# A hybrid diffusion layer on one core: the convolution's tiles are issued beside the last two RWKV pairs, and the order of issue is worked out with other durations

## The chip, the cores and the metric

One core of a Trainium2 chip runs the whole program. The metric is the device time of one execution, in microseconds (us); the time before is 1356.08 us, the median of three runs (1353.59 to 1361.63). The rows below come from one further execution that was profiled.

## What is computed

One layer of a hybrid backbone for 128 context and 512 latent tokens (T = 640 columns here, width D = 1024, all in float32). The reference, cut to what matters:

```python
xn = RMSNorm(x)*(1+sc1)+sh1
rkv, glu_in, gate_r, gate_c = split(xn @ w_in)
y_r = rwkv_branch(xn, rkv)      # two scans (forward, backward) per head, 8 heads of 64
y_c = conv_branch(glu_in)       # a * sigmoid(gt) -> depthwise conv of width 31 -> LayerNorm -> silu -> @ w_out_conv
x  += g1 * ((sigmoid(gate_r)*y_r + sigmoid(gate_c)*y_c) @ w_o)
x  += g2 * (relu(xn2 @ mlp_w1)**2 @ mlp_w2)
return RMSNorm(x)
```

## The kernel before

Activations lie with channels on the 128 partitions and tokens along the free axis. A dense product is done in split precision: a 128x512 piece of weights is split into a high part (ScalarE, `wh`) and a low part (VectorE, `wl`), and each of its four 128x128 blocks gives three matmuls of 320 columns (xh with wh, xl with wh, xh with wl). These are the rows `ps_mm<-xh_t,wh_t` and their like; one dense job is 48 of them, in two halves of the tokens.

The middle of the program is one loop over *lanes* (L1350 to L1364 in before), generators that record instructions for TensorE, VectorE and ScalarE in an order fixed by a small estimate: `now` is TensorE's time, `free` the other engines', `cost_v`, `cost_a` and `cost_g` the estimated durations, `mm` advances `now` by each matmul. A lane whose time has come is resumed, the more urgent first (table `URGENT`). Where none is ready, one matmul of the dense stream (`fill`) is recorded. `hungry` lets the dense stream go first where the estimate sees TensorE's clock about to fall. SyncE's DMA queue is not ordered by this loop. On the chip each engine works through its own list in order and waits where an operand is not there.

The lanes: `lora2_all`, `ada_all` (late modulation columns), and for each of four head pairs p `prep` (operands of the scan), `solve` (`gram` and `inverse`, long on VectorE), `builder` (five groups of scan matrices: a first block of matmuls that ends in bank `ps_t`, then one on `ps_a`, then one on `ps_a` and `ps_b`), `scan` (`chain`: ten steps in bank `ps_ad`, then `post`, the normalisation of the pair's output, whose result goes to DRAM as `out{p}`). `out_branch` reads the four `out{p}` back, splits them, and makes the side "r". `conv_all` is the convolution's lane: it waits until the gated inputs of the convolution are in DRAM, then `conv_tile` works on five tiles of 128 tokens: four transposes, for each 64-token row a matmul into frequencies (`cf_w`, 512 columns) and two VectorE products, an inverse transform (`cf_w`, 64 output rows), mean and variance, transposes back, tanh and scaling. Every one of these matmul groups writes the single bank `ps_t`, as do parts of the build, of the inverse and of `post`. The tiles' result makes the side "c".

The dense stream takes jobs in the order of `todo`: input projections, gates 8 to 15, two jobs of side "c", gates 0 to 7, then the four jobs of side "r" among the other two of "c". A job of a side that is not ready is passed over. After the loop come `w_o`, the MLP and the last norm, which the change leaves as they are.

In before, `conv_all` waits until pair 3 is inverted (`while 3 not in inverted`), and takes its tiles' space from the inverse (tags `prod`, `Nb`, `Gf`, `Gt`, `E`).

Of the kernel before, what the change touches and what calls it, by code (L numbers as in the profile page):

```python
# [17 lines left out]
P = 128  # L18
D = 1024
KD = D // P  # L20
T = 640
# [37 lines left out]
RAWS, SPLITS, SWITCH, EXTRA = ["ZB", "L"], ["N1"], 1, 0  # L59
# [11 lines left out]
TICK, ENTRY, QUOTA, CREDIT, DEBT = 3.413, 3060, 1.55, 200, 6000  # L71
# [7 lines left out]
def hybrid_step(ctx: ExitStack, tc: tile.TileContext, I, O):  # L79
# [115 lines left out]
    def mm(out, lhsT, rhs, start=True, stop=True, **kw):  # L195
        PE.matmul(out=out, lhsT=lhsT, rhs=rhs, start=start, stop=stop, **kw)  # L196
        cyc = math.prod(rhs.shape[1:]) * (1 if rhs.dtype == F32R else 2 if "is_transpose" in kw else 4)
        m = math.prod(lhsT.shape[1:])
        overlap = 128 // m if m < 128 else 128 // rhs.shape[0]
        cols = cyc * rhs.shape[0] / 128 * (1 if rhs.dtype == F32R else 0.5)  # L200
        gated["cols"] += cols
        gated["burst"] -= cols
        gated["credit"] = min(gated["credit"] + cols, CREDIT)
        kind = (m, rhs.shape[0], rhs.dtype)
        if kind != gated["kind"]:
            advance(now[0] + SWITCH * gated["drain"] / (2400 if gated["warm"] else 1200))
        gated.update(kind=kind, drain=0 if rhs.dtype == F32R else max(cyc, 256) - max(cyc / overlap, 64))
        advance(now[0] + (max(cyc / overlap, 64) + EXTRA) / (2400 if gated["warm"] else 1200))
        ready[out.name] = ("P", now[0] + SEM / 2)
        last[0] = now[0]  # L210
# [779 lines left out]
    def solve(p):  # L990
# [4 lines left out]
        inverted.add(p)  # L995

# [92 lines left out]
    def conv_all():  # L1089
# [6 lines left out]
        while 3 not in inverted:  # L1096
            yield 0.5
        ew = wt([P, 2 * P + W], "prod")[0:32]
        DMA.dma_start(out=ew[:, 0:2 * P], in_=I["ce"])
        DMA.dma_start(out=ew[:, 2 * P:], in_=I["cwb"])  # L1100
        yield 3.0
        for j in range(2):
            ps = bank("t")
            mm(ps, ew[:, P * j:P * j + P], ew[:, 2 * P:])
# [5 lines left out]
        us, tok = wt([P, 2, 4, P], "prod"), wt([P, 2, W], "Nb")  # L1110
        prods = [wt([P, 2, W], tag) for tag in ("Gf", "Gt")]

        def load(i):
            if i < 5:
                for j in range(4):
                    DMA.dma_start(out=us[:, i % 2, j], in_=dram(f"glu{j}")[:, P * i:P * i + P])

        load(0)
        yield 2.5
# [3 lines left out]
        places.extend(("Gf", "Gt"))  # L1123
        sides["c"] = Side(un, 8, merge_c, ("kS", "kS"))
        yield 2.5
        ready_sides.add("c")

    def conv_tile(i, u, tok, prods, un):

        ut, yn = tok[:, 0], tok[:, 1]  # L1130
        ps = bank("t")
        for j in range(4):
            mm(ps[:, P * j:P * j + P], u[:, j], ident)
        A.activation(ut, ps, AF.Copy)
        yield
        for r in range(2):
# [3 lines left out]
            V.scalar_tensor_tensor(out=prods[r][:, 0], in0=ps, scalar=cf[:, P + 384:P + 385], in1=cg[:, 0], op0=ALU.add, op1=ALU.mult)  # L1140
            V.tensor_tensor(out=prods[r][:, 1], in0=ps, in1=cg[:, 1], op=ALU.mult)
            yield
        ps = bank("t")
        for j in range(2):
            for r in range(2):
                o = P + 192 * j + 64
                if i < 4:
                    mm(ps[64 * r:64 * r + 64], cf[:, o:o + 64], prods[r][:, j], j == 0, j == 1)
                else:
                    mm(ps, cf[:, o - 64 * r:o - 64 * r + P], prods[r][:, j], (j, r) == (0, 0), (j, r) == (1, 1))  # L1150
        y = wt([P, W], "E")
        A.activation(y, ps, AF.Copy)
        yield
# [5 lines left out]
        V.tensor_scalar(out=yn, in0=y, scalar1=mv[:, 0:1], scalar2=r1, op0=ALU.subtract, op1=ALU.mult)  # L1159
        yield  # L1160
        ps = bank("t")
        for j in range(4):
            mm(ps[:, P * j:P * j + P], yn[:, P * j:P * j + P], ident)
        z, th = wt([P, 4, P], "E"), ut.rearrange("p (j t) -> p j t", j=4)
# [5 lines left out]
        V.scalar_tensor_tensor(out=z, in0=th, scalar=1.0, in1=z, op0=ALU.add, op1=ALU.mult)  # L1170
        yield
        h, l = (un[:, j, :, P * i:P * i + P] for j in range(2))
        A.activation(h, z, AF.Copy)
        yield
        V.tensor_tensor(out=l, in0=z, in1=h.bitcast(F32), op=ALU.subtract)
        yield
# [76 lines left out]
    def ada_all():  # L1253
        e = wt([P, 4, P], "ade")
        for c in range(16, 48):
            yield from ada_late(c, e)

# [383 lines left out]
```

## Time and profile before

| what | us |
|---|---|
| median of the runs | 1356.08 |
| the profiled execution | 1359.46 |
| its span, first to last instruction | 1357.4 |
| from 150 us to the last step of the last pair's chain | 521.4 |
| from there to the first product of a side | 93.3 |
| side products, to the first `w_o` matmul in another bank | 56.4 |
| `w_o`, MLP, last norm | 536.3 |

The stretches are cut at 150.0, 671.4, 764.7 and 821.1 us. In a row of the timeline stand start, duration, engine, source line, operation, output and inputs, and in brackets the idle time of the engine before it and what ended it. PEclk is TensorE's granted clock as a share of 2.4 GHz: 0.50 is the lower level, 1.2 GHz.

### The profile page before, as it was taken

Reading aid. Unit: us, or ns where it says so; the run is one execution under the profiler, and the core shown is the slowest. Engines: PE = TensorE matmul, PEld = TensorE weight load, DVE = VectorE, ACT = ScalarE, POOL = GpSimd, SP = SyncE. Lnnn points to the kernel's source line nnn. Section 1 sums busy time; section 2 is a strip of 40 time slices with the busy share of each in tenths; the row PEclk is TensorE's granted clock in tenths of the full one; section 3 lists DMA queues with packets and bytes.
Section 4 is the critical chain, followed back from the end, with each engine's and each line's share of the span. In section 5 each row is a group of like instructions: output and inputs, shape, how many; then the busy total and the mean of one; then the engine's idle time right before and its main releaser. Section 6 shows DMA issues by size and latency. Waiting matters only on the chain.

```text
span 1357.4 us, 29973 instructions
## 1 busy us (share of the span) xinstructions
PE 1228.3 (90%) x12790; PEld 1098.3 (81%) x12790; DVE 662.8 (49%) x1354; ACT 491.2 (36%) x1093; POOL 29.2 (2%) x30
## 2 busy tenths in 40 slices
PE   8999889989889998998755599999999999999996
PEld 5767787768778876886532589999999999999996
DVE  5426655656556454633432366574443443344344
ACT  4555244325433543343311323344431341242130
POOL 0000000010000000000000000000000000000000
PEclk9999889998989998998955699989999999999998
DMA  9475422324213212430100385212222222222222
GB/s 373 152 227 174 132 77 97 125 93 136 82 54 106 65 49 71 130 101 27 48 27 0 103 253 199 94 37 66 78 78 78 72 76 71 78 78 78 72 76 78
DMA packets 77780, 136.20 MB, mean 100 GB/s; under 512 B 10768, under 2 KB 27824, under 8 KB 77648
## 3 DMA queue, kind: packets, MB, share of 16 engines
q1 hardware_dynamic: 77648, 134.30, 30.1%
q8 instruction: 100, 1.64, 0.5%
q14 instruction: 32, 0.26, 0.1%
HBM read 113.03 MB, written 21.23 MB: 99 GB/s over the span
## 4 chain that ended last, share of the span: by engine, by line
PE 82%; DVE 6%; DMA 4%; ACT 4%; issue 4%; SPq 0%; POOL 0%; POOLq 0%; DVEq 0%; ACTq 0%
PE ps_mm L196 42%; PE ps_b L196 21%; PE ps_t L196 11%; PE ps_a L196 5%; PE ps_ad L196 3%; DMA adar_s<-in_adaw 2%; ACT S_w L108 1%; DVE Gt_w L108 1%; ACT Nb_w L108 1%; DMA z<-tmp 1%; DVE E_w L108 1%; DVE prod_w L108 1%; ACT tmp L108 1%; DVE Y_w L108 0%; DVE wl_t L108 0%
## 5 line engine op out<-in xcount | busy, mean ns | idle before, releaser
L196 PE MATMUL ps_mm<-xh_t,wh_t 128*128 128x320 f32 x680 | 226.5, 333 | 1.1 <-ACT tmp L108 1.0
L196 PE MATMUL ps_mm<-xh_t,wl_t 128*128 128x320 f32 x680 | 223.3, 328 | 1.2 <-DVE wl_t L108 1.2
L196 PE MATMUL ps_mm<-xl_t,wh_t 128*128 128x320 f32 x680 | 222.6, 327 | 0.0
L108 DVE TENSOR_TENSOR wl_t<-wr_t,wh_t 128x512 fp32r<-128x512 f32 x152 | 104.4, 687 | 108.9 <-ACT wh_t L108 108.8
L108 ACT ACTIVATE wh_t<-wr_t 128x512 fp32r<-128x512 f32 x152 | 95.5, 629 | 149.6 <-PE ps_b L196 106.6
L196 PEld LDWEIGHTS ps_mm<-xh_t,wh_t 128*128 128x128 f32 x680 | 133.5, 196 | 17.7 <-issue 12.0
L196 PEld LDWEIGHTS ps_mm<-xh_t,wl_t 128*128 128x128 f32 x680 | 133.7, 197 | 12.3 <-issue 8.1
L196 PEld LDWEIGHTS ps_mm<-xl_t,wh_t 128*128 128x128 f32 x680 | 134.0, 197 | 10.0 <-issue 7.8
L196 PE MATMUL ps_mm<-ARGH_t,wh_t 128*128 128x320 f32 x284 | 78.3, 321 | 11.7 <-ACT wh_t L108 11.0
L108 ACT ACTIVATE tmp<-ps_mm 128x320 f32<-128x320 f32 x80 | 34.9, 436 | 110.1 <-PE ps_mm L196 95.6
L196 PE MATMUL ps_mm<-ARGH_t,wl_t 128*128 128x320 f32 x212 | 67.6, 319 | 0.0
L196 PEld LDWEIGHTS ps_mm<-ARGH_t,wh_t 128*128 128x128 f32 x284 | 53.2, 199 | 12.5 <-ACT wh_t L108 11.3
L108 ACT ACTIVATE mwh<-wr_t 128x512 fp32r<-128x512 f32 x49 | 31.1, 635 | 74.0 <-PE ps_b L196 70.2
L108 DVE TENSOR_TENSOR tmp<-tmp 128x320 f32<-128x320 f32 x64 | 31.3, 489 | 43.2 <-ACT tmp L108 43.1
L108 DVE TENSOR_TENSOR mwl<-wr_t,mwh 128x512 fp32r<-128x512 f32 x49 | 33.9, 691 | 37.9 <-ACT mwh L108 37.8
L108 DVE SCALAR_TENSOR_TENSOR ARGH_t<-ps_mm,mod_t,ARGH_t 128x320 f32<-128x320 f32 (+2 forms) x45 | 22.6, 512 | 59.5 <-PE ps_mm L196 59.5
L196 PE MATMUL ps_mm<-xl,wh_t 128*128 128x320 f32 x140 | 44.1, 315 | 0.0
L196 PE MATMUL ps_b<-xl,wh_t 128*128 128x320 f32 x140 | 43.2, 309 | 0.0
L196 PE MATMUL ps_b<-ARGH_t,wl_t 128*128 128x320 f32 x140 | 43.0, 307 | 0.0
L196 PE MATMUL ps_b<-ARGH_t,wh_t 128*128 128x320 f32 x140 | 43.0, 307 | 0.0
L196 PEld LDWEIGHTS ps_mm<-ARGH_t,wl_t 128*128 128x128 f32 x212 | 41.7, 196 | 0.4 <-DVE wl_t L108 0.4
L196 PE MATMUL ps_ad<-M_w,S_w 128*64 128x64 f32 x320 | 19.1, 244 | 24.5 <-ACT S_w L108 23.0
(375 smaller groups left out, 3011.6 us busy)
## 6 DMA issues: line engine op xcount, KB each, us to landing
wr_t<-in_w SPq DMA_DIRECT2D x224, 256.0 KB, 2.6
adl_w<-in_adal SPq DMA_DIRECT2D x64, 256.0 KB, 3.3
adar_s<-in_adaw SPq DMA_DIRECT2D x16, 512.0 KB, 8.4
ARGH_t<-in_x SPq DMA_DIRECT2D x8, 640.0 KB, 6.2
z<-tmp SPq DMA_DIRECT2D x32, 160.0 KB, 2.9
gate<-tmp SPq DMA_DIRECT2D x32, 160.0 KB, 1.8
tA_t<-z SPq DMA_DIRECT2D x8, 320.0 KB, 3.2
ath_t<-z SPq DMA_DIRECT2D x8, 320.0 KB, 4.4
```

Of the source, the lines that this page charges most:

```text
L108: return f(*args, **kw)
L196: PE.matmul(out=out, lhsT=lhsT, rhs=rhs, start=start, stop=stop, **kw)
```

## The change

The convolution's tiles start earlier, as soon as pair 2 is prepared, pair 3's r and k are projected and the late modulation is done (`modulated`). Their space now comes from buffers that are free then (`kS`, `rS`, `adl`, `ade`). Each 64-token row of a tile has its own inverse transform right after its products, so that the two halves of the output, which stood next to one another in TensorE's order, now stand apart. A tile's result goes to DRAM (`conv{j}`); a new lane `conv_branch` reads it back once pair 2 is built, splits it and makes side "c". The bank stays `ps_t`. In the estimate, the costs of VectorE and ScalarE, of a fp32r matmul (`EXTRA`, 31 cycles more) and of going between fp32 and fp32r (`ENTER`, `LEAVE`) are changed, the time from a matmul to its reader is doubled (`SEM` for `SEM / 2`), and `QUOTA` goes from 1.55 to 1.25.

```diff
-TICK, ENTRY, QUOTA, CREDIT, DEBT = 3.413, 3060, 1.55, 200, 6000
+TICK, ENTRY, QUOTA, CREDIT, DEBT = 3.413, 3060, 1.25, 200, 6000
...
+EXTRA, ENTER, LEAVE = 31, 250, 220
...
     def cost_v(name, n, src, kw):
-        return 0.07 + 0.06 * aps_(kw, "scalar", "scalar1") + n / 960
+        return 0.155 + n / (480 if name == "tensor_tensor_scan" else 550 if name == "transpose" else 960)
...
-        return (0.08 if src[0].space == PSUM else 0.16) + 0.093 * aps_(kw, "scale", "bias") + n / 1400
+        return (0.16 if src[0].space == PSUM else 0.19) + 0.093 * aps_(kw, "scale", "bias") + n / 1180
...
-            advance(now[0] + SWITCH * gated["drain"] / (2400 if gated["warm"] else 1200))
+            enters = (rhs.dtype == F32R) - (gated["kind"] is not None and gated["kind"][2] == F32R)
+            advance(now[0] + (gated["drain"] + (0, ENTER, LEAVE)[enters]) / (2400 if gated["warm"] else 1200))
...
-        while 3 not in inverted:
+        while 2 not in prepared or (0, 3) not in rk or (1, 3) not in rk or not modulated:
             yield 0.5
...
-        while 2 not in built or 3 not in operated:
-            yield 0.3
-        un = st([P, 2, 4, T], "ARGH", 2, F32R)
+        pr = [wt([P, W], "adl", 2) for _ in range(2)]
         for i in range(5):
-            load(i + 1)
-            yield from conv_tile(i, us[:, i % 2], tok, prods, un)
+            for j in range(4):
+                DMA.dma_start(out=u[:, P * j:P * j + P], in_=dram(f"glu{j}")[:, P * i:P * i + P])
+            yield 2.5
+            yield from conv_tile(i, u, ut, pr)
+        spawn(conv_branch(), URGENT["branch"])
...
         for r in range(2):
...
             yield
+            ps = bank("t")
+            at, n = (lo, 64) if i < 4 else (slice(0, P), P)
+            for j in range(2):
+                o = P + 192 * j + 64 - (0 if i < 4 else 64 * r)
+                mm(ps[at], cf[:, o:o + n], pr[j], j == 0, j == 1)
...
+        for j in range(4):
+            DMA.dma_start(out=dram(f"conv{j}")[:, P * i:P * i + P], in_=z[:, j])
...
+    def conv_branch():
+
+        while 2 not in built or 3 not in operated:
+            yield 0.3
+        un = st([P, 2, 4, T], "ARGH", 2, F32R)
+        for j in range(4):
+            t = st([P, T], f"ath{j % 2}")
+            DMA.dma_start(out=t, in_=dram(f"conv{j}"))
+            yield 2.5 if j == 0 else 0.5
+            split(un[:, 0, j, :], un[:, 1, j, :], t)
+            yield "V"
+        sides["c"] = Side(un, 8, merge_c, ("kS", "kS"))
```

TensorE's list at the end of the last pair. Before, from the last two chain steps (`ps_ad`) on: `Y_w`, `pa_t` and `rh_t` belong to `post` of pair 3, `prod_w`, `Nb_w` and `cf_w` to the convolution, `ARGH_t` with `wh_t` to side "c".

```order
L196 MATMUL ps_ad<-S_w,M_w 64x64 x4
L196 MATMUL ps_ad<-M_w,S_w 64x64 x4
L196 MATMUL ps_t<-cst_t,Nb_w 128x128 x4
L196 MATMUL ps_t<-Y_w,cst_t 64x320 x4
L196 MATMUL ps_t<-cst_t,pa_t 128x2 x5
L196 MATMUL ps_t<-cst_t,prod_w 128x128 x4
L196 MATMUL ps_t<-cst_t,rh_t 64x128 x10
L196 MATMUL ps_t<-Nb_w,cf_w 128x512 x2
L196 MATMUL ps_t<-Gf_w,cf_w 64x512
L196 MATMUL ps_t<-Gt_w,cf_w 64x512
```

Two further tiles of the same kind follow before the first product of side "c". The same place now (`Gt_w` holds weights of side "c" here; the last row is the first product of side "r"):

```order
L197 MATMUL ps_mm<-ARGH_t,Gt_w 128x320 x5
L197 MATMUL ps_ad<-S_w,M_w 64x64 x4
L197 MATMUL ps_ad<-M_w,S_w 64x64 x4
L197 MATMUL ps_mm<-ARGH_t,Gt_w 128x320 x8
L197 MATMUL ps_t<-Y_w,cst_t 64x320 x2
L197 MATMUL ps_mm<-ARGH_t,Gt_w 128x320 x4
L197 MATMUL ps_t<-Y_w,cst_t 64x320 x2
L197 MATMUL ps_t<-cst_t,pa_t 128x2 x5
L197 MATMUL ps_t<-cst_t,rh_t 64x128 x10
L197 MATMUL ps_mm<-ARGH_t,wh_t 128x320 x2
```

No matmul of the convolution is left behind the chain; 84 of the 96 matmuls of the first two "c" jobs stand ahead of its last step, 12 among `post`.

TensorE's list at the inverse transform of a tile. Before, beside pair 3, with the two halves of the tile next to one another (`Gf_w`, `Gt_w` are their products) among gates:

```order
L196 MATMUL ps_mm<-xl_t,wh_t 128x320
L196 MATMUL ps_mm<-xh_t,wl_t 128x320
L196 MATMUL ps_t<-Gf_w,cf_w 64x512
L196 MATMUL ps_t<-Gt_w,cf_w 64x512
L196 MATMUL ps_t<-Gf_w,cf_w 64x512
L196 MATMUL ps_t<-Gt_w,cf_w 64x512
L196 MATMUL ps_mm<-xh_t,wh_t 128x320
```

Now, beside the build of pair 2 (rows `ps_t<-ARGH_t` are the end of the build's first block, `ps_a` its second block):

```order
L197 MATMUL ps_t<-cst_t,ARGH_t 64x64
L197 MATMUL ps_t<-ARGH_t 64x64
L197 MATMUL ps_t<-adl_w,cf_w 64x512 x2
L197 MATMUL ps_mm<-xl_t,wh_t 128x320
```

One half of the tile stands alone, and here, as at three more places, a step of the convolution stands directly behind the build's first block, where five or six dense matmuls stood in before.

## Rows read from the trace of the kernel before

**Rows 1.** The page: busy time, share of the span and instructions of each engine.

```profile
PE 1228.3 (90%) x12790; PEld 1098.3 (81%) x12790; DVE 662.8 (49%) x1354; ACT 491.2 (36%) x1093; POOL 29.2 (2%) x30
```

**Rows 2.** Windows: length, busy of PE, PEld, DVE, ACT, POOL, PEclk, DMA share, GB/s.

```profile
150.00:671.40 521.40, 470.52 (x7614) 401.49 (x7612) 282.77 (x593) 214.90 (x533) 18.49 (x16) 0.95 0.27 88
671.40:764.70 93.30, 46.67 (x133) 23.17 (x131) 30.97 (x59) 16.92 (x33) 3.97 (x4) 0.56 0.06 18
764.70:821.10 56.40, 53.74 (x337) 52.00 (x338) 33.59 (x66) 14.25 (x27) 0.00 (x0) 0.94 0.77 239
821.10:1357.40 536.30, 523.08 (x3553) 521.70 (x3552) 249.33 (x505) 170.39 (x333) 3.41 (x4) 0.98 0.24 79
```

**Rows 3.** Timeline of TensorE behind the chain's last step, 668 to 714 us.

```profile
670.97 0.45 PE L196 MATMUL ps_ad<-M_w,S_w 128*64 128x64 f32 x8 [0.38 <-ACT ade_t L108]
...
676.37 1.34 PE L196 MATMUL ps_t<-Y_w,cst_t 128*64 128x320 f32 x4 [3.87 <-DVE E_w L108]
...
686.47 1.98 PE L196 MATMUL ps_t<-cst_t,rh_t 128*64 128x128 f32 x16 [0.84 <-ACT Nb_w L108]
...
693.94 2.07 PE L196 MATMUL ps_t<-Nb_w,cf_w 64*128 64x512 f32 x2 [1.44 <-DVE Gf_w L108]
```

**Rows 4.** Timeline of VectorE in the same stretch: the steps of `post`.

```profile
671.77 0.29 DVE L108 TENSOR_TENSOR Y_w<-ps_ad,Y_w 128x128 f32<-128x128 f32 x1 [0.73 <-ACT Y_w L108]
...
690.02 0.35 DVE L108 SCALAR_TENSOR_TENSOR Y_w<-Y_w,par_t,ps_t 128x128 f32<-128x128 f32 x1 [0.79 <-PE ps_t L196]
...
693.80 0.88 DVE L108 SCALAR_TENSOR_TENSOR Y_w<-Y_w,par_t,pg_t 128x640 f32<-128x640 f32 x1
...
697.62 0.83 DVE L108 TENSOR_TENSOR Y_w<-Y_w,pg_t 128x640 f32<-128x640 f32 x1 [0.22 <-DMA pg_t<-g]
```

**Rows 5.** Timeline of SyncE's queue: the pair's output is stored; its landing.

```profile
698.47 0.32 SPq L1073 DMA_DIRECT2D out<-Y_w  x1
...
DMA to landing us min/median/max: 2.1/2.1/2.1
```

**Rows 6.** Timeline, all engines, 760 to 765 us: the end of the stretch.

```profile
760.37 1.06 SPq L1190 DMA_DIRECT2D ath_t<-out  x2
763.35 0.74 ACT L108 ACTIVATE ARGH_t<-ath_t 128x640 fp32r<-128x640 f32 x1 [3.24 <-DMA ath_t<-out]
...
764.66 0.90 PE L196 MATMUL ps_mm<-ARGH_t,wh_t 128*128 128x320 f32 x2 [11.00 <-ACT wh_t L108]
```

**Rows 7.** Timeline of TensorE where a tile runs among dense matmuls, 602 to 666 us.

```profile
602.96 1.16 PE L196 MATMUL ps_t<-cst_t,prod_w 128*128 128x128 f32 x8
603.87 0.39 PE L196 MATMUL ps_mm<-xh_t,wh_t 128*128 128x320 f32 x1
...
659.40 1.12 PE L196 MATMUL ps_t<-Nb_w,cf_w 64*128 64x512 f32 x2
660.45 0.41 PE L196 MATMUL ps_mm<-xh_t,wl_t 128*128 128x320 f32 x1
660.70 0.31 PE L196 MATMUL ps_mm<-xh_t,wh_t 128*128 128x320 f32 x1
660.85 0.31 PE L196 MATMUL ps_mm<-xl_t,wh_t 128*128 128x320 f32 x1
...
663.48 0.64 PE L196 MATMUL ps_t<-Gf_w,cf_w 128*64 128x512 f32 x1
663.49 0.64 PE L196 MATMUL ps_t<-Gt_w,cf_w 128*64 128x512 f32 x1
...
665.35 0.42 PE L196 MATMUL ps_mm<-xl_t,wh_t 128*128 128x320 f32 x1
```

**Rows 8.** Timeline, TensorE and VectorE: a build's first block ends and bank `ps_t` is read.

```profile
658.22 0.33 PE L196 MATMUL ps_t<-ARGH_t 64*64 64x64 f32 x3
...
658.58 0.69 DVE L108 TENSOR_TENSOR L_w<-ps_t,cst_t 128x512 f32<-128x512 f32 x1 [0.16 <-PE ps_t L196]
```

**Rows 9.** Waits of TensorE, 140 to 672 us: us in total, times, longest.

```profile
PE ps_ad L196 <- ACT S_w L108: 23.0, 32, 2.8
```

More of the change, by code (lines that the diff above doesn't have):

```diff
@@ L205, in mm @@
         if kind != gated["kind"]:
[L206 removed]
+            enters = (rhs.dtype == F32R) - (gated["kind"] is not None and gated["kind"][2] == F32R)
+            advance(now[0] + (gated["drain"] + (0, ENTER, LEAVE)[enters]) / (2400 if gated["warm"] else 1200))
         gated.update(kind=kind, drain=0 if rhs.dtype == F32R else max(cyc, 256) - max(cyc / overlap, 64))
[L208 to L209 removed]
+        advance(now[0] + (max(cyc / overlap, 64) + (EXTRA if rhs.dtype == F32R else 0)) / (2400 if gated["warm"] else 1200))
+        ready[out.name] = ("P", now[0] + SEM)
         last[0] = now[0]
@@ L995, in solve @@
         inverted.add(p)
+        if p == 3:
+            places.extend(("Gf", "Gt"))
     def builder(p):
@@ L1095, in conv_all, with conv_tile @@
                 yield 1.0
-        while 3 not in inverted:
+        while 2 not in prepared or (0, 3) not in rk or (1, 3) not in rk or not modulated:
             yield 0.5
[L1098 to L1101, printed above, removed]
+        u, ut = wt([P, W], "kS", 2), wt([P, W], "rS", 2)
         for j in range(2):
+            DMA.dma_start(out=u[0:32, 0:P], in_=I["ce"][:, P * j:P * j + P])
+            if j == 0:
+                DMA.dma_start(out=ut[0:32], in_=I["cwb"])
+            yield 3.0
             ps = bank("t")
-            mm(ps, ew[:, P * j:P * j + P], ew[:, 2 * P:])
+            mm(ps, u[0:32, 0:P], ut[0:32])
             A.activation(cg[:, j], ps, AF.Copy)
             yield
-        while 2 not in built or 3 not in operated:
-            yield 0.3
-        un = st([P, 2, 4, T], "ARGH", 2, F32R)
[L1110 to L1119, printed above, removed]
-        for i in range(5):
-            load(i + 1)
-            yield from conv_tile(i, us[:, i % 2], tok, prods, un)
[L1123 to L1130, printed above, removed]
+        pr = [wt([P, W], "adl", 2) for _ in range(2)]
+        for i in range(5):
+            for j in range(4):
[3 more added lines that the diff above has]
+        spawn(conv_branch(), URGENT["branch"])
+    modulated = []
+    def conv_tile(i, u, ut, pr):
         ps = bank("t")
         for j in range(4):
-            mm(ps[:, P * j:P * j + P], u[:, j], ident)
+            mm(ps[:, P * j:P * j + P], u[:, P * j:P * j + P], ident)
         A.activation(ut, ps, AF.Copy)
         yield
+        y = wt([P, W], "ade")
         for r in range(2):
@@ L1139, in conv_tile @@
             mm(ps, cf[lo, 0:P], ut[lo])
-            V.scalar_tensor_tensor(out=prods[r][:, 0], in0=ps, scalar=cf[:, P + 384:P + 385], in1=cg[:, 0], op0=ALU.add, op1=ALU.mult)
-            V.tensor_tensor(out=prods[r][:, 1], in0=ps, in1=cg[:, 1], op=ALU.mult)
+            V.scalar_tensor_tensor(out=pr[0], in0=ps, scalar=cf[:, P + 384:P + 385], in1=cg[:, 0], op0=ALU.add, op1=ALU.mult)
+            V.tensor_tensor(out=pr[1], in0=ps, in1=cg[:, 1], op=ALU.mult)
             yield
[L1143 to L1153, printed above, removed]
+            ps = bank("t")
[3 more added lines that the diff above has]
+                mm(ps[at], cf[:, o:o + n], pr[j], j == 0, j == 1)
+            if i == 4 and r:
+                V.tensor_tensor(out=y, in0=ps, in1=y, op=ALU.add)
+            else:
+                A.activation(y[at], ps[at], AF.Copy)
+            yield
         s6, mv, r1 = st([P, 6], "cs6"), st([P, 2], "cmv"), st([P, 1], "cr1")
@@ L1170, in conv_tile @@
         V.scalar_tensor_tensor(out=z, in0=th, scalar=1.0, in1=z, op0=ALU.add, op1=ALU.mult)
+        for j in range(4):
+            DMA.dma_start(out=dram(f"conv{j}")[:, P * i:P * i + P], in_=z[:, j])
         yield
[L1172 to L1176, printed above, removed]
+    def conv_branch():
[9 more added lines that the diff above has]
+        sides["c"] = Side(un, 8, merge_c, ("kS", "kS"))
+        yield 2.5
+        ready_sides.add("c")
     merged = []
@@ L1256, in ada_all @@
             yield from ada_late(c, e)
+        modulated.append(True)
     def fill():
```

8 lines of the change are left out of this document (4 added, 4 removed).

## The prediction

> **What bounds the kernel now.** I read the page first, then the windows, then the timeline of the stretch that stands out, then the waits. The page says that TensorE is busy 90% of the span [rows 1]; that is an average over stages that differ, which the windows part [rows 2]. From 821.1 us on, and from 764.7 to 821.1 us, TensorE loads weights 97% and 92% of the time at a clock of 0.98 and 0.94: there nothing but less work helps, and the change leaves both stages' kind of work alone. From 150 to 671.4 us dense matmuls fill what the lanes leave; TensorE is busy 470.5 of 521.4 us. Between them lie 93.3 us in which TensorE is busy 46.7 us, at a clock of 0.56, with 133 matmuls. This is the hole. It begins with the last step of pair 3's chain, 670.97 + 0.45 = 671.4 us [rows 3], and ends with the first product of side "c" at 764.66 us [rows 6]. In it stand `post` of pair 3 and three and a bit of the five tiles, each step waiting for the step before: the dense stream has nothing left, since the next jobs need the convolution.
>
> **What the change removes there.** All of the convolution leaves the hole. What stays is `post` and the way from its result to side "r". I add that up from the rows, without the tiles' pieces that stand between. Behind the chain's last step VectorE has the sums of `Y` done at 671.77 + 0.29 = 672.06 us [rows 4]; in the new list 8 dense matmuls stand ahead of `post`, at a pitch of 0.15 us [rows 7] 1.2 us, so `post` starts 1.2 us behind the chain's end. From its first matmul, 676.37 us [rows 3], to the end of its last short step on VectorE, 690.02 + 0.35 us [rows 4], are 14.0 us; a group of four transposes of a tile lies in there, but while `post` waits for something else anyway. Then 0.9 us for the next step (693.80 us, 0.88), and 697.62 - 694.68 = 2.9 us for a load, and 0.8 us for the last product [rows 4]; the store goes out at 698.47 us [rows 5]. Sum: 1.2 + 14.0 + 0.9 + 2.9 + 0.8 + 0.1 = 19.9 us from the chain's end to the store. The store lands after 2.1 us [rows 5]; then the last of the four results is read back, 763.35 - 760.37 = 3.0 us, and split, and the weights' split stands behind it on ScalarE: 764.66 - 763.35 = 1.3 us to the first product [rows 6]. With 0.1 us of issue that is 6.5 us. The hole is then 19.9 + 6.5 = 26.4 us for 93.3 us: **66.9 us less**. The weights of the first "r" job are issued ahead of the store on SyncE's queue, so they don't wait for it; the next ones stand behind the read of the store and are needed 14 us later.
>
> **What it moves.** The first two "c" jobs, 96 matmuls, go from behind the hole to before it. Behind the hole 96 x 0.147 = 14.1 us fall away (56.4 us for 384 products there is the same 0.147 us each [rows 2]). Ahead of it 84 of them come, 12.3 us; the other 12 lie within `post` and are in the 1.2 us above or beside its waits.
>
> The tiles go beside pairs 2 and 3, where TensorE has other work, so their TensorE time is paid there. Prices at full clock, from start to the start of the next dense matmul [rows 7]: four transposes 603.87 - 602.96 = 0.91 us; a matmul into frequencies 660.45 - 659.40 = 1.05 us; an inverse of both halves 665.35 - 663.48 = 1.87 us, and there the matmuls of the two halves run at the same time (663.48 and 663.49 us). In the new list a half stands alone, so I take 1.87 us for each half: the same four passes one behind the other. Each piece also makes the next dense matmul 0.1 us longer (660.70 - 660.45 = 0.25 for 0.15 us). A tile is then 2 x 0.91 + 2 x 1.05 + 2 x 1.87 + 6 x 0.1 = 8.3 us, five are 41.3 us. Before, 11.6 us of tiles were already ahead of 671.4 us (one whole, 1.82 + 2.10 + 1.87 + 0.5 = 6.3 us, and one without its last transposes, 5.3 us). So 29.7 us are added.
>
> At four places a piece stands directly behind a build's first block. It writes `ps_t`, which VectorE still reads until 658.58 + 0.69 = 659.27 us, while the block's last matmul starts at 658.22 and takes 0.33 us [rows 8]: 0.8 us each, 3.2 us; with two such places in `post` of pair 2, 4.5 us. What is queued behind is the build itself, and behind it the chain. Against this, the last 4 us before the chain's end, in which TensorE now waits for single steps without dense matmuls between, get dense ones: 4 us less.
>
> **Waits that stay.** The largest named wait of TensorE ahead of the hole is that of the chain's second product for ScalarE, 23.0 us in 32 times [rows 9]. Nothing of the lane's own order there changes, so I count no gain. Tile work on VectorE and ScalarE (VectorE is busy 283 of 521 us, ScalarE 215 [rows 2]) lies beside dense matmuls at no cost; if it stood alone it would cost what it costs in the hole. The 20 stores of the tiles and four reads go through a queue whose transfers fill 27% of the DMA engines [rows 2]; one that waits for VectorE holds up the weights behind it, and the weights' low part costs TensorE next to nothing today. The new numbers of the estimate reorder all of the middle; I take zero for that, with both signs open.
>
> **The sum.** The hole -66.9; "c" -14.1 and +12.3; tiles +29.7; bank +4.5; end of the chain -4. That is -38.5 us. The profiled execution took 1359.46 us, its span 1357.4; so the changed kernel's would be 1321 us. The median of the runs, 1356.08 us, lies 3.4 us lower: **1317 us** on that footing.
>
> **Rivals.** *TensorE has room before the hole.* For it: TensorE loads weights there 401 of 521 us, 77%, against 97% where it is full [rows 2]. If tiles and "c" jobs fell into that room, of +46.5 us some 20 would be left: 1317 - 27 = 1290 us. Against it: dense matmuls stand ready there all the time, so what is open is open because the list's order makes TensorE wait [rows 9], and other dense matmuls don't fill it either. I give it 0.17.
>
> The Trainium skill (Perfetto Trace Analysis, Identifying the Most-Contended Engine) holds the busy share of weight loads for the better measure of how near TensorE is to its bound, and matmul busy time for a bad one. By that this rival would be the forecast; the trace shows the gap between the two shares, 77 against 90%, but not that a piece placed there costs nothing.
>
> *The one bank holds the list up.* All 32 pieces of the convolution write `ps_t`, and so do build, inverse and `post`. In the hole a piece that directly follows another one's reading waits 1.44 us [rows 3]. If half of them met this, 16 x 1.44 = 23 us instead of 4.5: 1317 + 18 = 1335 us. Against it: between most pieces stand 6 or 7 dense matmuls, about 1 us, and the longest reading I see is two VectorE steps. 0.18.
>
> The Trainium skill (Perfetto Trace Analysis, Optimizing Tensor Performance) says that independent matmul groups should rotate through different PSUM banks, so that emptying one overlaps the next group's matmuls. It speaks against this change, which spreads one bank's groups among another user's groups; the row with 1.44 us agrees, at the place where nothing else stands between.
>
> *Slower.* The clock. The pieces among dense matmuls ran at the upper level, at 0.56 on average a frequency matmul takes 2.07 us for 1.12 [rows 3, 7]. Ahead of the hole the clock is 0.95 [rows 2]. Fewer dense matmuls a stretch and more waits could let it fall there. A fall by 0.01 means 2% more of the stretch at half speed, which loses about 1%, some 5.6 us of 560 us; to eat the 38.5 us it must fall from 0.95 to 0.88, and to be slower by over 0.5% (6.8 us, about what a measurement of this kernel can tell from no change) to 0.87: 1363 us and up. Against it: the stretch keeps its dense matmuls and gains 84, and the hole's low clock comes from its waits. 0.05.
>
> *The gain doesn't come.* If some wait of a new kind (a store of a tile that holds back weights, a chain that gets its steps later) puts the chain's end 35 us further back than I count, the time is within 0.5%: 1349 to 1363 us. 0.05.
>
> **How the numbers follow.** Forecast 0.55: 1317 us, between 1305 and 1330, as the reordering gives or takes some 12 us. Room 0.17: 1285 to 1304. Bank 0.18: 1330 to 1349. No gain 0.05. Slower 0.05. The range 1294 to 1340 us takes the forecast whole, and somewhat over half of room and bank; that leaves about 2 in 10 outside. Faster by over 0.5% 0.90 (0.55 + 0.17 + 0.18), within 0.05, slower 0.05.
>
> **What would show it.** In the changed kernel's windows: the hole, from the chain's last step to the first product of side "r", some 26 us; the chain's end at 671.4 + 42.5 = 714 us; 288 products behind the hole in some 42 us; the rest as before, 536 us. The room rival shows as a chain's end before 700 us, the bank as waits of `ps_t` for VectorE or ScalarE between 400 and 700 us that add up to over 20 us, the clock as under 0.90 there. I am wrong in the price of half an inverse if two of its matmuls start together; I am wrong in `post` if the hole is over 35 us.

## The result

The changed kernel takes 1341.93 us (median of four runs, 1337.01 to 1347.35), the kernel before, run beside it, 1356.6 us (1353.59 to 1361.63): a ratio of 0.9893, 95% interval 0.9848 to 0.9938. It is faster, as forecast, but by 14.7 us and not by 39, and 1.9 us outside the range. The profiled execution took 1337.01 us (span 1334.7), where I had 1321.

The page of the changed kernel says nearly what [rows 1] say (TensorE busy 1217.7 us for 1228.3, in as many matmuls): the work is the same.

The windows of the changed kernel, cut as in [rows 2] at the chain's end, the end of the hole and the end; the columns are length, busy time of PE, PEld, DVE, ACT and POOL (with instructions), granted clock, DMA share, GB/s:

```profile
150.00:735.30 585.30, 517.83 (x7840) 432.33 (x7837) 314.16 (x653) 235.28 (x576) 20.20 (x19) 0.96 0.29 90
735.30:759.30 24.00, 7.46 (x51) 5.14 (x51) 7.88 (x14) 4.32 (x8) 1.97 (x1) 0.63 0.29 85
```

```profile
759.30:1334.70 575.40, 560.65 (x3792) 557.89 (x3792) 275.52 (x557) 181.31 (x355) 3.40 (x4) 0.98 0.27 90
```

The hole is 24.0 us long for 93.3, where I had 26.4. What lies behind it is 575.4 us for 56.4 + 536.3 = 592.7 us [rows 2], 17.3 us less where I had 14.1. Both of these steps held. What failed is the chain's end: 735.3 us, where I had 714. The timeline of TensorE in the changed kernel, from the chain's last step on, shows the hole's two ends and `post` between them; it answers to [rows 3, 6]:

```profile
734.82 0.45 PE L197 MATMUL ps_ad<-M_w,S_w 128*64 128x64 f32 x8 [0.38 <-ACT ade_t L109]
...
736.57 0.76 PE L197 MATMUL ps_t<-Y_w,cst_t 128*64 128x320 f32 x4
...
746.73 0.70 PE L197 MATMUL ps_t<-cst_t,rh_t 128*64 128x128 f32 x4 [0.93 <-DVE Y_w L109]
759.29 0.90 PE L197 MATMUL ps_mm<-ARGH_t,wh_t 128*128 128x320 f32 x2 [11.87 <-ACT wh_t L109]
```

So the question is one of 21 us ahead of the chain's end. The waits of TensorE there (what waits, for whom, us in total, times, longest) have three rows that grew: the chain's second product for ScalarE, 29.6 for the 23.0 us of [rows 9]; bank `ps_t` for VectorE's reading of a build's block (`L`), which was next to nothing; and `ps_t` for a tile's scaling (`ade_w`), which the kernel before does not have there.

```profile
PE ps_ad L197 <- ACT S_w L109: 29.6, 32, 3.2
...
PE ps_t L197 <- DVE L_w L109: 6.3, 8, 0.8
PE ps_t L197 <- DVE ade_w L109: 4.4, 2, 2.2
```

The row of `L` in the kernel before:

```profile
PE ps_t L196 <- DVE L_w L108: 0.4, 1, 0.4
```

### The profile page after: what moved, and what is told of

It is laid out like the page before. It is cut to its first block, busy times and chain, and to the rows that moved or that the text cites. A ratio compares the mean times of both kernels' runs of the same rounds, so it can differ in the third digit from the quotient of the medians.

```text
span 1334.7 us, 30014 instructions
## 1 busy us (share of the span) xinstructions
PE 1217.7 (91%) x12790; PEld 1093.0 (82%) x12790; DVE 662.6 (50%) x1354; ACT 490.6 (37%) x1096; POOL 28.9 (2%) x30
## 5 line engine op out<-in xcount | busy, mean ns | idle before, releaser
L197 PE MATMUL ps_mm<-xh_t,wl_t 128*128 128x320 f32 x664 | 219.9, 331 | 0.9 <-DVE wl_t L109 0.8
L197 PE MATMUL ps_mm<-xh_t,wh_t 128*128 128x320 f32 x664 | 218.4, 329 | 1.1 <-ACT tmp L109 0.6
L197 PE MATMUL ps_mm<-xl_t,wh_t 128*128 128x320 f32 x664 | 216.2, 326 | 0.0
L197 PEld LDWEIGHTS ps_mm<-xh_t,wl_t 128*128 128x128 f32 x664 | 130.2, 196 | 18.6 <-issue 15.4
L197 PEld LDWEIGHTS ps_mm<-xh_t,wh_t 128*128 128x128 f32 x664 | 130.6, 197 | 14.4 <-issue 9.6
L197 PEld LDWEIGHTS ps_mm<-xl_t,wh_t 128*128 128x128 f32 x664 | 130.3, 196 | 14.0 <-issue 12.7
L197 PE MATMUL ps_mm<-ARGH_t,wh_t 128*128 128x320 f32 x268 | 74.8, 321 | 12.4 <-ACT wh_t L109 11.9
L197 PEld LDWEIGHTS ps_mm<-ARGH_t,wh_t 128*128 128x128 f32 x268 | 49.9, 198 | 13.8 <-ACT wh_t L109 12.3
L197 PE MATMUL ps_ad<-M_w,S_w 128*64 128x64 f32 x320 | 19.3, 246 | 31.1 <-ACT S_w L109 29.6
L109 ACT ACTIVATE ade_w<-ps_t 128x128 f32<-128x128 f32 (+2 forms) x41 | 14.2, 346 | 86.6 <-PE ps_t L197 86.5
L197 PEld LDWEIGHTS ps_ad<-M_w,S_w 128*64 128x64 f32 x320 | 13.5, 146 | 36.9 <-ACT S_w L109 34.0
```

Of the source, the lines that this page charges most:

```text
L109: return f(*args, **kw)
```

## The experiments

Beside these rows I use sums by kind of matmul ("in sum"): the time from each matmul's start to the start of the next one, added up over a kind from 120 us to the chain's end, worked out from the starts in the trace. "Build's first block" is in these sums `ps_b<-cst_t,vS_w`, `ps_a` and `ps_b<-M_w,ARGH_t`, `ps_t<-cst_t,ARGH_t` and `ps_t<-ARGH_t`. A block's last matmul takes in the wait of whatever stands behind it.

### The two halves of the change apart

My first theory was that the new numbers of the estimate, for which I had counted zero, cost the 21 us. The change splits in two: the convolution's edits with the old numbers, and the new numbers with the old convolution. The edit of the first, against the changed kernel, cut (the cost of ScalarE and of a matmul go back too):

```diff
-RAWS, SPLITS = ["ZB", "L"], ["N1"]
-EXTRA, ENTER, LEAVE = 31, 250, 220
+RAWS, SPLITS, SWITCH, EXTRA = ["ZB", "L"], ["N1"], 1, 0
-TICK, ENTRY, QUOTA, CREDIT, DEBT = 3.413, 3060, 1.25, 200, 6000
+TICK, ENTRY, QUOTA, CREDIT, DEBT = 3.413, 3060, 1.55, 200, 6000
...
-        return 0.155 + n / (480 if name == "tensor_tensor_scan" else 550 if name == "transpose" else 960)
+        return 0.07 + 0.06 * aps_(kw, "scalar", "scalar1") + n / 960
...
-        ready[out.name] = ("P", now[0] + SEM)
+        ready[out.name] = ("P", now[0] + SEM / 2)
```

> The kernel before with the convolution's edits alone; the old numbers of the estimate and the old 1.55 of dense work per step stay. My theory: the 21.6 us that the chain's end came too late are the order's doing, which the new numbers change in all of the middle. By it the convolution alone is worth what I worked out, some -38 us: chain's end at 710 to 720 us, time 1317 to 1325 us, faster than the changed kernel. Rival (the convolution's pieces beside pairs 2 and 3 cost more than I priced them, by bank and waits): chain's end at 725 us or later, time 1335 to 1345 us, as the changed kernel or slower. Second rival: with the old numbers the list puts the pieces where their inputs are not ready, and the time is above 1345 us.

Measured: 1352.02 us, ratio 0.9963 (0.9931 to 0.9994). The first theory falls in this form: the convolution alone is worth a third of a per cent. The time is where the second rival had it, above 1345 us, but the cause that the traces show is another. The window from its chain's end at 691.6 us to its first side product:

```profile
691.60:754.70 63.10, 26.68 (x126) 18.45 (x125) 19.52 (x35) 12.86 (x24) 2.89 (x2) 0.71 0.26 79
```

With the old numbers the list still puts a fifth of the convolution behind the chain's end, and no product of "c" ahead of it.

The other half, against the kernel before:

```diff
-RAWS, SPLITS, SWITCH, EXTRA = ["ZB", "L"], ["N1"], 1, 0
+RAWS, SPLITS = ["ZB", "L"], ["N1"]
+EXTRA, ENTER, LEAVE = 31, 250, 220
...
-TICK, ENTRY, QUOTA, CREDIT, DEBT = 3.413, 3060, 1.55, 200, 6000
+TICK, ENTRY, QUOTA, CREDIT, DEBT = 3.413, 3060, 1.25, 200, 6000
```

(with the new `cost_v`, `cost_a`, matmul times and `ready` of the change).

> The kernel before with the new numbers of the estimate and the 1.25 of dense work per step, and the convolution as before. My theory (the new order of the middle costs time ahead of the chain's end): slower than the kernel before by 5 to 20 us, 1361 to 1376 us. Rival (the new numbers are worth nothing or a gain, and the loss is the convolution's): 1335 to 1358 us. With the convolution's edits alone, the two differences from the kernel before should add up to the -14.7 us of both within 8 us; if not, they work on each other.

Measured: 1362.06 us, ratio 1.0045 (1.0013 to 1.0077): slower, at the low end of the theory. Windows, to its chain's end and through its hole, and a row of its waits:

```profile
150.00:689.30 539.30, 477.10 (x7741) 408.19 (x7735) 289.79 (x603) 221.82 (x549) 18.25 (x16) 0.96 0.27 88
689.30:772.80 83.50, 41.83 (x116) 19.27 (x114) 27.87 (x53) 13.91 (x27) 4.10 (x4) 0.54 0.05 17
```

```profile
PE ps_t L197 <- DVE L_w L109: 6.3, 8, 0.8
```

The hole is 9.8 us shorter, since more tile work stands ahead of it (4.0 us of it in sum), and still the time is 4.4 us longer. So the new order costs some 4.4 + 9.8 - 4.0 = 10 us ahead of the chain's end. This is an estimate: the 4.4 us is a difference of medians, the other two come from one profile each.

The traces show where it arises. The first chain step of all starts at 210.23 us in the kernel before, at 220.33 in the changed kernel and at 227.29 here; from there to the last pair's chain's end are 461.2, 515.0 and 462.0 us. So this list loses nothing behind the first chain step. Ahead of it, where no tile runs, the traces of both kernels with the new numbers have 86 more matmuls than that of the kernel before, 72 of the late modulation and 14 dense, and TensorE waits 4.2 us for ScalarE once. The rows are of the kernel before, then of the changed kernel:

```profile
210.23 0.45 PE L196 MATMUL ps_ad<-S_w,M_w 128*64 128x64 f32 x8
```

```profile
125.72 0.90 PE L197 MATMUL ps_mm<-ARGH_t 64*128 64x320 f32 x1 [4.25 <-ACT kS_w L109]
...
220.33 0.45 PE L197 MATMUL ps_ad<-S_w,M_w 128*64 128x64 f32 x8
```

Of the 17 us here some 7 are this execution's: up to there its list is that of the changed kernel, whose step comes at 220.33 (more on that in the last section). In the four kernels with the old numbers and 1.45 or 1.55 the step comes at 207.9 to 210.2 us, in the eight with the new numbers at 214.1 to 235.7.

The wait for `L` is as large without the convolution's edits as with them, so it comes with the numbers: build's first block is 13.5 us dearer in sum here, 12.2 us in the changed kernel, and 4.3 us with the convolution alone, in whose list no piece of the convolution stands directly behind it. The two halves add up to -1.2 us and the whole gives -14.7: they work on each other, since of the three kernels only the one with both has all five tiles ahead of the chain's end.

### Four tanh, four scalings, one bank

The long waits of the chain for ScalarE, above 2.5 us, stand at a tile's tanh. The timeline of the changed kernel, all engines, at one of them:

```profile
509.44 0.46 ACT L109 ACTIVATE rS_w<-ps_t,hlnb_t,hlng_t 128x128 f32<-128x128 f32 x1 [1.69 <-PE ps_t L197]
...
509.56 0.45 PE L197 MATMUL ps_ad<-S_w,M_w 128*64 128x64 f32 x8
509.93 0.41 DVE L109 TENSOR_SCALAR ade_w<-ps_t,par_t 128x128 f32<-128x128 f32 x1 [2.56 <-ACT rS_w L109]
510.38 0.46 ACT L109 ACTIVATE rS_w<-ps_t,hlnb_t,hlng_t 128x128 f32<-128x128 f32 x1 [0.48 <-DVE ade_w L109]
510.87 0.41 DVE L109 TENSOR_SCALAR ade_w<-ps_t,par_t 128x128 f32<-128x128 f32 x1 [0.53 <-ACT rS_w L109]
...
512.25 0.46 ACT L109 ACTIVATE rS_w<-ps_t,hlnb_t,hlng_t 128x128 f32<-128x128 f32 x1 [0.48 <-DVE ade_w L109]
512.61 0.54 ACT L109 ACTIVATE S_w<-ps_ad 64x128 f32<-64x128 f32 x2
...
513.20 0.70 PE L197 MATMUL ps_ad<-M_w,S_w 128*64 128x64 f32 x8 [3.19 <-ACT S_w L109]
```

Each tanh (ScalarE) waits for the scaling ahead of it (VectorE), and each scaling for its tanh: both read `ps_t`, and the program lets them at it one after the other. Four of each take 4 x 0.94 = 3.7 us on both queues, and the chain's copy of `S`, whose product starts at 509.56 us, comes to its turn at 512.61. TensorE has nothing else in its list there and waits 3.19 us. The edit issues the four tanh first:

```diff
             A.activation(th[:, j], b, AF.Tanh, scale=hlng[:, j:j + 1], bias=hlnb[:, j:j + 1])
+        for j in range(4):
+            b = ps[:, P * j:P * j + P]
             V.tensor_scalar(out=z[:, j], in0=b, scalar1=pc("conv_ln_g", j), scalar2=pc("conv_ln_b", j), op0=ALU.mult, op1=ALU.add)
```

> The changed kernel with a tile's four tanh on ScalarE issued ahead of the four scalings on VectorE; before, each alternates with the other on one bank and holds ScalarE's queue for 3.7 us, behind which the chain's copies of S stand. Theory (ScalarE's queue is what lengthens the chain's long waits, 2.7 to 3.4 us at three places): those waits fall to 0.9 us, chain's end 3 to 6 us earlier, time 1336 to 1339 us. Rival (other jobs on ScalarE take their place, or the chain waits for VectorE next): within 2 us of 1341.9 us.

Measured: 1327.82 us, ratio 0.9778 (0.9731 to 0.9825), 14.1 us below the changed kernel: more than I expected. The same place in its timeline:

```profile
505.95 1.51 ACT L109 ACTIVATE rS_w<-ps_t,hlnb_t,hlng_t 128x128 f32<-128x128 f32 x4 [1.69 <-PE ps_t L197]
...
506.08 0.45 PE L197 MATMUL ps_ad<-S_w,M_w 128*64 128x64 f32 x8
507.34 0.55 ACT L109 ACTIVATE S_w<-ps_ad 64x128 f32<-64x128 f32 x2
507.50 1.36 DVE L109 TENSOR_SCALAR ade_w<-ps_t,par_t 128x128 f32<-128x128 f32 x4 [3.62 <-ACT rS_w L109]
...
507.95 0.45 PE L197 MATMUL ps_ad<-M_w,S_w 128*64 128x64 f32 x8 [1.42 <-ACT S_w L109]
```

TensorE's order is that of the changed kernel but for two rows, so the traces can be laid side by side. The chain's end is at 724.2 us for 735.3, and the 11.1 us arise in pair 2 and at the start of pair 3, where the tiles run: 1.77 us at each of two waits like this one, 0.7 to 1.4 us at each of five other places, four of them in or at the inverse, which waits for VectorE (some of it given back in between), and the rest with a clock that is higher by 0.03 in that stretch. The changed kernel first, then this one, 460 to 580 us:

```profile
460.00:520.00 60.00, 51.92 (x897) 43.80 (x898) 31.76 (x54) 29.00 (x65) 1.79 (x3) 0.94 0.30 91
520.00:580.00 60.00, 49.05 (x731) 37.35 (x728) 29.49 (x55) 23.31 (x63) 0.54 (x1) 0.97 0.14 45
```

```profile
460.00:520.00 60.00, 54.98 (x936) 45.45 (x934) 32.95 (x58) 32.11 (x74) 1.80 (x3) 0.97 0.28 87
520.00:580.00 60.00, 51.14 (x814) 38.51 (x814) 33.17 (x62) 24.20 (x64) 0.55 (x1) 1.00 0.19 58
```

Is this a property of the new order only? The same edit on the convolution with the old numbers, where the chain's waits for ScalarE are no longer than before:

> The kernel before with the convolution's edits alone, and the four tanh first. Four tiles stand beside the chain there. Theory (taking turns on one bank costs 2.2 us or more for each tile that runs beside a chain): 6 to 11 us less than the 1352.0 us without it, 1341 to 1346 us. Rival (it costs only where a chain's copy stands behind the four tanh on ScalarE, which in this list it doesn't: waits of the chain for ScalarE are 23.2 us there, as before): within 3 us of 1352.0 us.

Measured: 1338.4 us, ratio 0.9877 (0.9818 to 0.9936), 13.6 us below its own base, and more than either expectation; the rival falls. Of the five tiles three have their tanh ahead of the chain's end (the expectation counted four). Its chain's end is at 677.4 us for 691.6. In this profile only one wait of the chain is 1.77 us shorter; the rest comes in smaller pieces and with a clock of 0.96 for 0.94 ahead of the chain's end.

```profile
150.00:677.40 527.40, 474.88 (x7610) 397.30 (x7608) 292.79 (x615) 218.37 (x542) 19.42 (x18) 0.96 0.26 85
```

How the 13.6 us divide between waits and clock I can't tell; that taking turns causes both is shown by the edit, which moves five rows of TensorE's order and else only the order of the eight steps.

### Pieces directly behind a build's block

In the changed kernel nine pieces (three of the late modulation, two others, four of the convolution) stand directly behind a build's first block and wait some 0.9 us each for the bank, 8 us in all. The first attempt holds every lane that writes `ps_t` until the estimate has its last reader done:

```diff
+                if any(t_bank[0] and a.name == t_bank[0] for a in src):
+                    t_free[0] = max(t_free[0], free[key] + SEM / 2)
...
-        return next((l for l in lanes if l[0] <= now[0] and (l[1] or dense)
+        return next((l for l in lanes if l[0] <= now[0] and (l[1] or dense) and (l[3] not in on_t or t_free[0] <= now[0])
...
```

> The changed kernel with one more rule in the order: a lane that writes the bank ps_t isn't resumed until the estimate has the bank's last reader done. Theory (about nine pieces directly behind a build's first block wait 1.0 us each for the bank): gaps behind the block vanish, chain's end 5 to 10 us earlier, time 1332 to 1337 us. Rival (TensorE then waits elsewhere for the same time, since the lanes are late by the same amount): time within 3 us of the changed kernel's 1341.9 us.

Measured: 1368.3 us, ratio 1.0071 (1.0045 to 1.0097), above theory and rival. The nine waits are gone, and one of 23 us has come, of a tile's transposes for a VectorE that is deep in an inverse; the chain ends at 765.9 us.

```profile
PE ps_t L204 <- DVE Gt_w L111: 23.1, 1, 23.1
```

The second attempt, with the four tanh first, lets only the reading behind the block count, with the same test in the choice of the next lane:

```diff
             V.tensor_tensor(out=L, in0=pl, in1=mask_a.unsqueeze(2).to_broadcast([P, 2, GC, P]), op=ALU.mult)
+            t_free[0] = t + 1.0
...
```

> The kernel with the four tanh first, and one more rule in the order: the lanes that write the bank ps_t wait, in the estimate, until VectorE has read it behind build's first block; other readers of the bank don't count. The nine pieces that stand directly behind such a block are gone. Theory (each of the nine costs 0.9 us and the rest of the list stays as good): chain's end 8 us earlier than with the four tanh first alone, 716 us for 724.2 us, time 1318 to 1322 us. Rival (the pieces are put later in the list and what waits for them waits as long, as with the wider rule, where one wait of 23 us for VectorE arose): within 4 us of 1327.8 us or slower, with new waits of TensorE that make up for the nine.

Measured: 1336.35 us, ratio 0.9863 (0.98 to 0.9926), 8.5 us above the kernel with the four tanh alone, as the rival had it; the two intervals still overlap, so it is not faster, and not surely slower. Build's block is 5.9 us cheaper in sum, and the rest of the list dearer. The third comes to no piece behind a block by another number, again with the four tanh first:

```diff
-TICK, ENTRY, QUOTA, CREDIT, DEBT = 3.413, 3060, 1.25, 200, 6000
+TICK, ENTRY, QUOTA, CREDIT, DEBT = 3.413, 3060, 1.4, 200, 6000
```

> The changed kernel with the four tanh first and 1.40 for 1.25 of dense work per step. In its list no piece stands directly behind a build's block, and 48 products of side c stand ahead of the chain's end for 84. Theory (the nine pieces behind the block cost 8 us): build's first block at 50 us in sum for 60.5 us, time 1318 to 1323 us for the 1327.8 us of 1.25. Rival (a list with more dense work per step pays in other places, above all in chain steps that come later): within 4 us of 1327.8 us or above it.

Measured: 1331.26 us, ratio 0.9833 (0.98 to 0.9866), within the rival's 4 us. Build's block is 55.2 us in sum for 60.5, and the time is no better. Three times the waits went and the time did not: each wait is real, but a list made without them had others. What one such piece costs the whole I have not measured.

### The dense work per step

```diff
-TICK, ENTRY, QUOTA, CREDIT, DEBT = 3.413, 3060, 1.25, 200, 6000
+TICK, ENTRY, QUOTA, CREDIT, DEBT = 3.413, 3060, 1.55, 200, 6000
```

in the changed kernel, and nothing else:

> The changed kernel with one number of the estimate put back, the dense work per step, 1.25 to 1.55. In its list 18 of the 30 matmuls into frequencies and back stand behind the chain's end again and no product of side c ahead of it. Theory (this number decides whether the convolution gets in beside the chains; the pieces directly behind a build's block, now eleven, come from the other numbers): hole of 60 us or more, time 1345 to 1365 us. Rival (the hole's tiles are paid back by an earlier chain's end, since they cost the same anywhere): chain's end at 690 us or earlier and time 1330 to 1345 us.

Measured: 1404.34 us, ratio 1.0378 (1.0313 to 1.0443). The theory had the direction and not the size: its hole is longer than that of the kernel before.

```profile
701.10:811.50 110.40, 52.16 (x123) 22.59 (x121) 30.57 (x56) 16.99 (x31) 3.60 (x4) 0.56 0.16 48
```

### The hole that is left

In the kernel with the four tanh first the hole is 23.8 us with TensorE busy 7.5 of them. Holding the first two "c" jobs for it:

```diff
-todo += [(lambda: "c" in ready_sides, lambda j: side_products("c", j), j, [B_OC + j]) for j in range(2)]
+todo += [(lambda: "c" in ready_sides and 3 in chained, lambda j: side_products("c", j), j, [B_OC + j]) for j in range(2)]
```

> The kernel with the four tanh first, and the first two jobs of side c (96 products, 14.1 us) held until the last pair's chain is issued, so that they stand in the hole of 24 us instead of ahead of it; the order ahead of them stays otherwise. Theory (the hole is empty of other work, and the list before it has dense matmuls to spare): the chain's end comes 8 to 14 us earlier, the hole gets no longer, time 1314 to 1320 us. Rival (without these products the last groups of the chain wait in the open, since the dense matmuls run out before): chain's end 0 to 4 us earlier, time 1324 to 1328 us.

Measured: 1331.15 us, ratio 0.9827 (0.9775 to 0.988): 3 us above the base, which the intervals can't tell from it; the gain of the theory is not there. The chain's end comes 0.7 us earlier in the profiles, 7.9 us if the first chain step, 7.2 us later in this execution, is taken off; but the hole is 32.4 us:

```profile
723.50:755.90 32.40, 21.64 (x134) 19.30 (x130) 13.16 (x24) 6.38 (x12) 2.29 (x1) 0.82 0.57 177
```

```profile
740.69 0.44 PE L197 MATMUL ps_t<-cst_t,rh_t 128*64 128x128 f32 x4 [0.85 <-DVE Y_w L109]
```

The products stand among `post`'s steps and hold them up (its last group starts 17.2 us behind the chain's end, for 11.4), and when side "r" is at last on its way nothing is left to do beside it.

The old numbers leave another filling: with 1.45 for 1.55, the convolution's edits and the four tanh first, all tiles stand ahead of the chain's end and 185 dense matmuls are left for behind it, ahead of the "c" jobs. Against the convolution with the old numbers and the tanh first:

```diff
-TICK, ENTRY, QUOTA, CREDIT, DEBT = 3.413, 3060, 1.55, 200, 6000
+TICK, ENTRY, QUOTA, CREDIT, DEBT = 3.413, 3060, 1.45, 200, 6000
```

> The kernel before with the convolution's edits, the four tanh first, the old numbers of the estimate, and 1.45 for 1.55 of dense work per step. In its list all five tiles stand ahead of the chain's end, one piece directly behind a build's block, and 185 dense matmuls (some 27 us) are left for the hole. Theory (the new numbers' own order of pairs 0 and 1 costs 14 to 18 us and isn't needed; a hole filled with dense matmuls costs only what post's steps wait behind them): first chain step at 208 us or earlier, chain's end at 670 to 680 us, hole 32 to 42 us, time 1305 to 1322 us. Rival (dense matmuls in the hole hold up post by as much as they bring, as the held products of side c did): hole of 50 us or more, time 1325 to 1338 us.

Measured: 1313.72 us (six runs, 1305.56 to 1320.6), ratio 0.9688 (0.965 to 0.9726): 40 us below the kernel before and 28 us below the changed kernel, as the theory had it in time, chain's end and hole (its first chain step is at 210.1 us, for 208). Its windows around the chain's end, and two rows of its waits:

```profile
150.00:679.50 529.50, 477.48 (x7572) 389.46 (x7572) 300.38 (x634) 222.74 (x553) 20.35 (x19) 0.95 0.25 83
679.50:714.10 34.60, 31.97 (x225) 29.73 (x224) 15.21 (x24) 12.84 (x24) 2.48 (x1) 1.00 0.60 198
```

```profile
PE ps_ad L196 <- ACT S_w L108: 23.4, 32, 1.6
...
PE ps_t L196 <- DVE L_w L108: 0.9, 2, 0.8
```

The stretch from the chain's end to the first side product is 34.6 us long, but TensorE is busy in 32.0 of them: 2.6 us idle for 16.3 us with the four tanh first and the new numbers. It ends with the "c" jobs, which need nothing of `post`, and "r" is ready when they are done. The clock in it is 1.00, the upper level throughout. Not all of the 44.7 us by which the chain ends earlier (679.5 for 724.2) is gain: what lies behind that stretch is 589.6 us for 573.7, since the "c" jobs are there now, and 11.0 us of the 44.7 stand already at the first chain step (210.1 for 221.1). The run changes the order as a whole, so it doesn't show what the filled hole is worth alone.

And the same with 1.35 (the edit against the kernel with 1.45):

```diff
-TICK, ENTRY, QUOTA, CREDIT, DEBT = 3.413, 3060, 1.45, 200, 6000
+TICK, ENTRY, QUOTA, CREDIT, DEBT = 3.413, 3060, 1.35, 200, 6000
```

> The same with 1.35. In its list again all five tiles stand ahead of the chain's end and 150 dense matmuls are left for the hole, but nine pieces stand directly behind a build's block instead of one. Theory (each costs 0.9 us of the chain's time): build's first block is 7 to 8 us dearer in sum than with 1.45, and the time 5 to 12 us longer than with 1.45. Rival (the nine waits are taken from waits that would come anyway): build's block dearer, but the time within 4 us of that with 1.45.

Measured: 1319.87 us, ratio 0.9735 (0.9703 to 0.9766), 6.2 us above 1.45. Build's block is 58.9 us in sum for 52.4. That is what the theory said, but the intervals touch, and this list differs in more than the nine places: 150 dense matmuls are left for 185, and the first chain step comes at 219.6 us for 210.1, which is more than the whole difference. Against the three lists above it settles nothing about the price of one.

## Why the prediction was wrong

**The hole.** Right: 24.0 us for 26.4, with `post` starting 1.3 us behind the chain's end for my 1.2. **"c" behind the hole.** Right: 17.3 us less for 14.1.

**Tiles and "c" ahead.** Right in size: the tiles' groups are 26.2 us dearer in sum, for 29.7; the products of "c" 14.5, for 12.3. The halves of an inverse do run one behind the other. **The end of the chain.** Not 4 us: in the 12 us ahead of the chain's end TensorE is idle 2.1 us in the kernel before and 1.0 us in the changed one, some 1 us less.

**"Tile work on VectorE and ScalarE [...] lies beside dense matmuls at no cost; if it stood alone it would cost what it costs in the hole."** This is the step that failed first. The tiles' tanh and scalings hold both queues, and behind them wait the chain and the inverse, which TensorE's list puts directly next. Issuing the tanh first gives back 11.1 us of chain's end and 14.1 us of time. The pattern stood in the trace of the kernel before. The longest of the 32 waits of [rows 9], 2.8 us, is this one: the tanh of its first tile run beside the chain, and the chain's copy of `S` stands behind them:

```profile
631.38 0.46 ACT L108 ACTIVATE Nb_w<-ps_t,hlnb_t,hlng_t 128x128 f32<-128x128 f32 x1 [2.70 <-PE ps_t L196]
...
634.20 0.46 ACT L108 ACTIVATE Nb_w<-ps_t,hlnb_t,hlng_t 128x128 f32<-128x128 f32 x1 [0.48 <-DVE E_w L108]
634.55 0.54 ACT L108 ACTIVATE S_w<-ps_ad 64x128 f32<-64x128 f32 x2
...
635.14 0.69 PE L196 MATMUL ps_ad<-M_w,S_w 128*64 128x64 f32 x8 [2.83 <-ACT S_w L108]
```

I counted no change for that row because the lane's own order stays, and did not ask what its longest wait stood behind. The same four tanh are in the hole, at 728.87, 729.80, 730.74 and 731.68 us, scalings between; I had read them only as part of a stretch that goes away, and not as work that moves to where two other lanes use the same queues. My "longest reading" of the bank, two VectorE steps, was wrong for the same reason: the tanh and scalings of a tile read it for 3.7 us. I had listed shares (VectorE 283 of 521 us [rows 2]); a share says nothing about what stands behind a step of 3.7 us.

The Trainium skill (PSUM — Partial Sum Buffer, PSUM bank collisions raise a hardware error) says that two engines must not be at the same partitions of one bank at once, two readers included, and that the compiler therefore adds a dependency between them. The trace agrees with the dependency: 0.48 and 0.53 us of waiting ahead of each turn. I had weighed the next matmul group against a bank's reader, and not two readers against each other.

**"The new numbers of the estimate reorder all of the middle; I take zero for that."** The second step that failed: some 10 us, by the numbers alone. In the profiles the 21 us by which the chain's end is later than my 714 part at the first chain step: 10.1 us are there already (220.3 for 210.2, one profile each, and such places differ by some 7 us between executions), and 11.3 come behind it (515.0 us from there to the chain's end, where I had 461.2 + 42.5 = 503.7). With the four tanh first that stretch is 503.1 us. That it then meets my sum to 1 us is partly luck: build's first block is 12.2 us dearer in sum where I had 4.5 for the bank, and other terms are cheaper than I had them. Less the 2.4 and 3.2 us that the hole and "c" gave beyond my sum, the chain's end makes the 16 us by which the profiled execution missed. The other 9 us of the miss of 1341.9 - 1317 = 25 us are, but for rounding, no mechanism: the profiled execution of the kernel before lies 3.4 us above its median, that of the changed kernel 4.9 us below.

My bank term of 4.5 us was right in the price of a piece: of the eight waits for `L`, 0.8 us each, four are the convolution's, the 3.2 us that I had for them. The others belong to the new order. And zero hid more than a loss: the dense work per step decides whether the tiles get in. At 1.55 they don't, with the old numbers or the new; at 1.25, and with the old numbers at 1.45, they do.

**The rivals.** "One bank holds the list up" gave 1330 to 1349 us, and the time lies in there, but not by its mechanism. Its mark was over 20 us of waits of `ps_t` for VectorE or ScalarE between 400 and 700 us; the changed kernel's waits there are 13.0 us:

```profile
PE ps_t L197 <- DVE ade_w L109: 4.4, 2, 2.2
PE ps_t L197 <- DVE L_w L109: 3.9, 5, 0.8
PE ps_t L197 <- DVE Y_w L109: 2.6, 4, 0.9
...
PE ps_t L197 <- ACT pa_t L109: 0.9, 1, 0.9
PE ps_t L197 <- DVE kk_t L109: 0.9, 1, 0.9
...
PE ps_t L197 <- DVE adl_w L109: 0.3, 1, 0.3
```

The bank did cost, most of it through its two readers' queues, where TensorE's waits carry other names (`S_w`). "Room before the hole" fell: the chain's end came later, not earlier. The clock ahead of the chain's end is 0.96, so "slower by the clock" did not come.

**What stays open.** Which of the new numbers brings the first chain step 10 us later, and how much of the gain from the tanh is clock. The list with the old numbers and 1.45 is the best found, and no rule is known by which a number near it would be as good: 1.35, 1.45 and 1.55 gave 1319.9, 1313.7 and 1338.4 us.

## What to carry to other kernels

Before moving work into a stretch where "other engines have room", go through its steps on those engines and look at what will stand behind each of them in the same queue; the two engines that read one bank took turns here, and issuing all of one engine's reads before the other's gave 14 us on two lists. Read what the longest wait of a row stands behind before you count the row as unchanged. A change of the numbers that set an order was not zero here: run it alone, and run the rest without it. And of the two fillings of the hole tried here, dense matmuls that need nothing of `post`, with the "c" jobs behind them, did better than the "c" jobs put among `post`'s steps; but those two lists differ in more than that.

## What was not expected of the hardware

Executions of nearly the same program differ at its start. The first 120 us of the kernel with the four tanh first, and of the one with the "c" jobs held, whose lists are the same up to there:

```profile
0.00:120.00 120.00, 106.64 (x737) 76.66 (x737) 48.06 (x105) 57.42 (x130) 3.32 (x6) 0.97 0.67 233
```

```profile
0.00:120.00 120.00, 109.50 (x700) 79.20 (x701) 43.54 (x97) 55.01 (x124) 3.33 (x6) 0.90 0.64 226
```

A granted clock of 0.97 and 0.90, means over stretches at 2.4 and at 1.2 GHz, and a first chain step at 221.1 and 228.4 us. The lateness stays to the last pair. So a place in time of one profile can't be compared with another's to better than some 7 us; a difference within a stretch can.
